# The first value block between the two key blocks, and the output product split around the second eight heads' sums, in a two-layer trunk

## The chip, the cores and the metric

One core of one Trainium2 chip. The metric is device time in microseconds for one execution of the whole program (both layers, 256 frames); lower is better. Before the change: 611.75 us, the median of 3 runs (611.36 to 612.37).

## What is computed

A trunk of two layers on `x` of 256 frames by 1024, float32. Layer 0 mixes frames by differential attention, layer 1 by sparse attention with a choice of keys; each mixer and each MLP (4096 wide, squared ReLU) is preceded by an RMS norm and followed by a residual. The change is in layer 1's mixer:

```python
def dsa_attention(h, w_in, cq_g, w_uq, w_uq_idx, q_g, k_g, w_out, cos, sin):
    proj = h @ w_in
    c_q, k, v, k_idx, w_idx = split(proj)          # 256, 1024, 1024, 64, 8 columns
    c_q = rms_norm(c_q, cq_g)
    q = c_q @ w_uq                                 # 16 heads of 64
    q_idx = rope(c_q @ w_uq_idx)                   # 8 index heads of 64
    k_idx = rope(rms_norm(k_idx))
    q = rope(rms_norm(q, q_g)) * 64 ** -0.5
    k = rope(rms_norm(k, k_g))
    # per block of 128 queries
    score = einsum('bqh,bqhk->bqk', w_idx, relu(q_idx . k_idx))   # masked by chunks of 64
    vals, idx = top_k(score, 64)
    s = q . k[idx]
    p = softmax(s over the chosen keys)
    return (p @ v[idx]) @ w_out
```

The kernel doesn't gather: it turns the top-k choice into a mask over all keys (`smask`) and computes dense scores.

## The kernel before, in words

**Precision by three products.** Every float32 weight matrix is streamed from memory in units of 128 x 2048 (1 MB). `unit` (L126) loads one to `raw` on SP's queue, makes its rounded part `whi` on ScalarE (L141) and the rest `wlo` on VectorE (L142), in two pieces of 1024 columns each. There are three `raw` buffers and four of `whi` and `wlo`, so a unit's split waits until the matmuls on the unit four places before it are done. A product is then three matmuls into one PSUM bank (`mm3`, L145; L146, L148, L150). `project` (L236) multiplies the normed input `h` by one block of 512 columns: two units, 48 matmuls of 512 columns. An `acc` PSUM bank is held for each of the two row tiles.

**Order of the weights.** `_weights` lays the units out in the order of their use: for the sparse layer the index and compressed-query columns, keys 0, keys 1, the query matrix (one unit), values 0, values 1, the output matrix (four units), then the MLP.

**Sparse attention.** `compress` and `index` (L676) compute the index queries and keys, their scores (L732) and the choice: for each of two query tiles eight rounds of a maximum of eight (L741) and its removal (L742) on VectorE. Meanwhile `project` makes keys 0 and 1 (each eight heads) and the query matrix gives queries 0 and 1 (one unit, 12 matmuls for each eight heads, 24 in all). After each, `qk_post` (L347) copies PSUM to `qn` (L354), squares (L356), reduces (L357), scales the keys (L364), applies rotary (L342 to L345, on VectorE), transposes on TensorE (L374) and copies the result (L377). `qn` has two buffers.

Then, for each half of the heads, `dsa_probs` (L771) takes four pairs of heads: score matmuls (L390), mask and minimum (L401), exponential on ScalarE (L412), division (L786, L788), transposes (L419) and copies to `aT` (L421). `dsa_out` (L791) multiplies by the values `vt` (L799, L800) and splits the result into the output product's operand `o` (L804 on ScalarE, L805 on VectorE); one call covers four heads, two calls one half. `v_part` (L554) projects one half of the values and copies it to `vt` (L558). `out_proj` (L430) multiplies `o` by the output matrix unit by unit: units 0 and 1 need the first half's `o`, units 2 and 3 the second's; each unit is 24 matmuls. Before each unit it drives the generators listed for it to their end (`needs`).

**What sets the order.** Python generators (`spawn`, `need`, `tick`, L92 to L118) fix the order in which instructions are traced; `PAUSE` (L41) gives the number of matmuls after which a waiting piece is traced. The framework then writes each engine's list at build time: an instruction traced earlier goes first among those that it takes to be ready, so an engine's list is not the traced order. On the chip every engine works through its list in order. The order traced before, for the sparse layer: keys 0 and their post-work, keys 1 and theirs, queries 0, queries 1, then for each half: probabilities, value block of that half, weighted sums; then the output product. The lines just there are

```python
    for half in range(2):
        aTs = []
        probs = spawn(dsa_probs(half, aTs))
        v_part(half, h, srow)
        need(probs)
        for i in range(2):
            dsa_out(2 * half + i, aTs[4 * i:4 * i + 4])
    h = new_h()
    out_proj(o, take() + take(), h, C_NORM + 24)
```

Of the kernel before, what the change touches and what calls it, by code (L numbers as in the profile page):

```python
# [25 lines left out]
C_NORM = 0  # L26
# [10 lines left out]
            0.0014142135623842478, 0.00027424818836152554, 5.3182957344688475e-05, 1.0313385246263351e-05]  # L37

PAUSE = {"idx scores 1": 1, "idx transposes 0": 1, "idx transposes 1": 36, "q1 transposes 0": 1,  # L41
         "out0": 1, "out1": 2, "out2": 24, "out3": 27}
# [3 lines left out]
def trunk(ctx: ExitStack, tc: tile.TileContext, x_in, pos_in, pack_in, wf, out):  # L46
# [13 lines left out]
    def acc():  # L60
        return psum.tile([128, 512], F32, name="acc", bufs=4)
# [36 lines left out]
    def advance(e, to_end=False):  # L98
        was, inside[0] = inside[0], True
        while e in side and (to_end or e[0] <= 0):  # L100
            try:
                e[0] = next(e[1])
            except StopIteration:
                side.remove(e)
        inside[0] = was

    def spawn(gen):
        e = [0, gen]
        side.append(e)
        advance(e)  # L110
        return e

    def need(*es):
        for e in es:
            advance(e, True)
# [10 lines left out]
    def unit(cols=2048, dmas=1, pieces=1, between=None):  # L126
        raw = wraw.tile([128, 2048], F32, name="raw")
        hi = wsp.tile([128, 2048], F32R, name="whi")
        lo = wsp.tile([128, 2048], F32R, name="wlo")
        src = bass.AP(tensor=wf.tensor, offset=wf.offset + off[0], ap=[[cols, 128], [1, cols]])  # L130
        off[0] += 128 * cols
        step = cols // dmas
        for i in range(dmas):
            c = slice(i * step, (i + 1) * step)
            nc.sync.dma_start(raw[:, c], src[:, c])
            if between is not None and i == 0:
                between()
        step = cols // pieces
        for i in range(pieces):
            c = slice(i * step, (i + 1) * step)  # L140
            nc.scalar.activation(hi[:, c], raw[:, c], AF.Copy)  # L141
            nc.vector.tensor_tensor(lo[:, c], raw[:, c], hi[:, c].bitcast(F32), op=OP.subtract)  # L142
        return hi[:, :cols], lo[:, :cols]

    def mm3(ps, ah, al, wh, wl, first, last):  # L145
        mm(ps, ah, wh, start=first, stop=False)  # L146
        tick()
        mm(ps, ah, wl, start=False, stop=False)  # L148
        tick()
        mm(ps, al, wh, start=False, stop=last)  # L150
        tick()
# [79 lines left out]
    def lhs(h, kt, t):  # L231
        hi, lo = h[kt // 4][:2]
        c = slice(t * 128, t * 128 + 128)
        return hi[:, kt % 4, c], lo[:, kt % 4, c]
# [195 lines left out]
    def out_proj(o, us, h, gc, needs=((),) * 4):  # L430


        ps = [[acc() for _ in range(2)] for _ in range(2)]
        for u, (wh, wl) in enumerate(us):
            need(*needs[u])
            wh = wh.rearrange("p (k n) -> p k n", n=D)
            wl = wl.rearrange("p (k n) -> p k n", n=D)
            for n in range(2):
                for t in range(2):
                    c = slice(n * 512, n * 512 + 512)  # L440
                    for i in range(2):
                        k = u * 2 + i
                        ah, al = lhs(o, k, t)
                        mm3(ps[t][n], ah, al, wh[:, i, c], wl[:, i, c], k == 0, k == 7)
                    if u == 3:
                        for j in range(2):
                            c = slice(n * 512 + j * 256, n * 512 + j * 256 + 256)
                            nc.vector.tensor_tensor(x[t][:, c], ps[t][n][:, j * 256:j * 256 + 256], x[t][:, c],
                                                    op=OP.add)
                            make_h(h, gc, t, n, (j,))  # L450
# [71 lines left out]
    h = new_h()  # L522
# [8 lines left out]
    srow, s2 = row_scale(1)  # L531
# [22 lines left out]
    def v_part(half, h, srow):  # L554
        ps = [acc() for _ in range(2)]
        project(ps, h, quad(take()), 512)
        for t in range(2):
            nc.scalar.activation(vt[:, t, half * 512:half * 512 + 512], ps[t], AF.Copy, scale=srow[:, t:t + 1])  # L558

    o = new_h()  # L560
# [60 lines left out]
    def take():  # L621
        return ready.pop(0) if ready else pair()

    pr = [[] for _ in range(4)]
    probs, outs = [], []
# [11 lines left out]
    h = new_h()  # L637
# [3 lines left out]
    h = h1  # L641
# [15 lines left out]
    srow, s2 = row_scale(2)  # L657
# [93 lines left out]
    def post(res, *a):  # L751
        res += yield from qk_post(*a)

    posts = []
    for n in range(2):
        ps = [acc() for _ in range(2)]
        project(ps, h, quad(take()), 512)
        posts.append(spawn(post(kTs[n], ps, s2c, scon, 3, 1, 0, (C_GT + 3, C_GT + 3), f"k{n}")))
    uq = [a.rearrange("p (k n) -> p k n", n=D) for a in unit(pieces=2)]
    for n in range(2):  # L760
        ps = [acc() for _ in range(2)]
# [7 lines left out]
    o = new_h()  # L769

    def dsa_probs(half, out):  # L771

        need(chosen, posts[half], posts[2 + half])
        rs = qTs[half][2]
        z = tiny.tile([128, 8, 2], F32, name="dz")
        st = {}
        for p in range(5):
            yield pause(f"probs {half}{p}")
            if p < 4:
                st[p] = scores(qTs[half][p // 2], kTs[half][p // 2], p % 2, smask)  # L780
            if p > 0:
                for r, (s, mn) in enumerate(st.pop(p - 1)):
                    hd = 2 * p - 2 + r
                    e = expo(s, mn, rs[:, :, hd], [z[:, hd, t:t + 1] for t in range(2)])
                    rz = tiny.tile([128, 2], F32, name="rz")
                    nc.vector.reciprocal(rz, z[:, hd])  # L786
                    for t in range(2):
                        nc.vector.tensor_scalar(e[:, TS[t]], e[:, TS[t]], rz[:, t:t + 1], None, op0=OP.mult)  # L788
                    out.append(to_keys(e))

    def dsa_out(g, aTs):  # L791
        ops = wk()
        for p in range(2):
            c = p * 256
            for r in range(2):
                rows = slice(64 * r, 64 * r + 64)
                a = aTs[2 * p + r]
                vc = (4 * g + 2 * p + r) * 64
                mm(ops[rows, c:c + 256], vt[:, 0, vc:vc + 64], a[:, 0:256], start=True, stop=False)  # L799
                mm(ops[rows, c + 128:c + 256], vt[:, 1, vc:vc + 64], a[:, 256:384], start=False, stop=True)  # L800
        k = 2 * g
        oh = o[k // 4][0][:, k % 4:k % 4 + 2].rearrange("p a b -> p (a b)")
        ol = o[k // 4][1][:, k % 4:k % 4 + 2].rearrange("p a b -> p (a b)")
        nc.scalar.activation(oh, ops, AF.Copy)  # L804
        nc.vector.tensor_tensor(ol, ops, oh.bitcast(F32), op=OP.subtract)  # L805

    for half in range(2):
        aTs = []
        probs = spawn(dsa_probs(half, aTs))
        v_part(half, h, srow)  # L810
        need(probs)
        for i in range(2):
            dsa_out(2 * half + i, aTs[4 * i:4 * i + 4])
    h = new_h()
    out_proj(o, take() + take(), h, C_NORM + 24)

    def store(t, n, j):
        if (t, n) != (1, 1) and j == 0:
# [13 lines left out]
def _weights(i):  # L832

    parts = []
    w = i["diff_w_in"][0]
    q, k, v = w[:, :1024], w[:, 1024:2048], w[:, 2048:]

    def add(m, rows):
        for r in range(0, m.shape[0], rows):
            parts.append(_tiles(m[r:r + rows]))  # L840

    def a(j):
        add(np.concatenate([q[:, 256 * j:256 * j + 256], k[:, 256 * j:256 * j + 256]], axis=1), 512)

    def mlp(w1, w2):
        def up(b):
            for s in range(2):
                parts.append(_tiles(w1[:, 512 * b + 256 * s:512 * b + 256 * s + 256]))

        up(0)  # L850
        for b in range(8):
            if b < 7:
                up(b + 1)
            add(w2[512 * b:512 * b + 512], 256)

    a(0)
    a(1)
    a(2)
    a(3)
    add(v[:, :512], 512)  # L860
    add(v[:, 512:], 512)
    add(i["diff_w_out"][0], 256)
    mlp(i["mlp_w1"][0], i["mlp_w2"][0])
    w = i["dsa_w_in"][0]
    c = np.concatenate([w[:, :256], w[:, 2304:]], axis=1)
    parts.append(_tiles(c[:768]))
    parts.append(np.concatenate([_tiles(m).reshape(128, -1) for m in (c[768:], i["dsa_w_uq_idx"][0])], axis=1).reshape(-1))
    add(w[:, 256:768], 512)
    add(w[:, 768:1280], 512)
    parts.append(_tiles(i["dsa_w_uq"][0]))  # L870
    add(w[:, 1280:1792], 512)
    add(w[:, 1792:2304], 512)
    add(i["dsa_w_out"][0], 256)
    mlp(i["mlp_w1"][1], i["mlp_w2"][1])
    return np.concatenate(parts)
# [44 lines left out]
```

## Time and profile before

| | |
|---|---|
| runs | 611.36, 611.75, 612.37 us |
| the profiled execution | 611.71 us, its span 609.2 us |
| TensorE (PE) busy | 595.2 us, 98% of the span |
| VectorE (DVE) busy | 428.7 us, 70% |
| ScalarE (ACT) busy | 368.5 us, 60% |
| GpSimd (POOL) busy | 15.9 us, all in the first 50 us |
| sparse attention | about 308 to 426 us of the span |

PE's busy time is modelled from overlapping matmuls, so the distance between the starts of neighbouring matmuls says more than their durations. In a row of the timeline the first number is the start, the second the length, `xN` merges N neighbours, and the bracket at the end is the idle time before it and what ended it.

### The profile page before, as it was taken

The numbers are of one execution on the slowest core, as the hardware profiler recorded it, in microseconds if no ns is written. First come the engines' busy times: TensorE is split into PE (matmuls) and PEld (weight loads), VectorE is DVE, ScalarE is ACT, GpSimd is POOL, SyncE is SP. The second block draws the span as 40 slices with busy tenths as digits, with TensorE's granted clock in tenths as the row PEclk, the third lists the DMA queues.
The fourth block names the chain that finished last, engine by engine and source line by source line (L and its number), as shares of the span: only waits on it lengthen the run. The fifth ranks groups of instructions, "written<-read, shape, count | busy, mean of one in ns | idle before, by whom it ended". The sixth has DMA issues, their size and how long they took to land.

```text
span 609.2 us, 8462 instructions
## 1 busy us (share of the span) xinstructions
PE 595.2 (98%) x3064; PEld 490.0 (80%) x3064; DVE 428.7 (70%) x1067; ACT 368.5 (60%) x720; POOL 15.9 (3%) x53
## 2 busy tenths in 40 slices
PE   8899999999999999999999899999999999999997
PEld 7677768888888888888787686768888888888886
DVE  5698986489566567557588999775886566665552
ACT  6788987577445445444397579794854454455430
POOL 5400000000000000000000000000000000000000
PEclk9899999999999999999999999999999999999999
DMA  8464343435645554554554216414475555555301
GB/s 314 180 257 165 138 157 132 176 109 210 218 176 207 205 165 183 208 192 149 197 178 169 70 69 207 140 69 139 139 230 194 197 206 169 186 200 203 143 1 69
DMA packets 16025, 102.29 MB, mean 168 GB/s; under 512 B 1904, under 2 KB 2416, under 8 KB 4336
## 3 DMA queue, kind: packets, MB, share of 16 engines
q1 hardware_dynamic: 15696, 101.62, 47.5%
q8 instruction: 24, 0.39, 0.3%
q10 hardware_dynamic: 288, 0.13, 0.1%
q14 instruction: 17, 0.14, 0.1%
HBM read 100.70 MB, written 1.05 MB: 167 GB/s over the span
## 4 chain that ended last, share of the span: by engine, by line
PE 82%; DVE 10%; ACT 3%; POOL 2%; issue 2%; DVEq 0%; POOLq 0%; ACTq 0%
PE wk L469 18%; PE acc L150 15%; PE acc L148 15%; PE acc L146 15%; PE wk L470 9%; DVE wlo L142 4%; DVE s L401 2%; PE wk L419 2%; PE acc L469 1%; PE wk L390 1%; PE wk L223 1%; ACT whi L141 1%; PE wk L374 1%; PE acc L470 1%; DVE score L742 1%
## 5 line engine op out<-in xcount | busy, mean ns | idle before, releaser
L142 DVE TENSOR_TENSOR wlo<-raw,whi 128x1024 fp32r<-128x1024 f32 (+2 forms) x210 | 229.8, 1116 | 119.1 <-ACT whi L141 118.9
L141 ACT ACTIVATE whi<-raw 128x1024 fp32r<-128x1024 f32 (+2 forms) x210 | 197.8, 974 | 95.4 <-issue 46.1
L146 PE MATMUL acc<-whi,act 128*128 128x512 f32 (+1 forms) x504 | 200.7, 399 | 2.0 <-ACT whi L141 2.0
L148 PE MATMUL acc<-wlo,act 128*128 128x512 f32 (+1 forms) x504 | 199.2, 395 | 0.8 <-DVE wlo L142 0.8
L150 PE MATMUL acc<-whi,act 128*128 128x512 f32 (+1 forms) x504 | 199.2, 395 | 0.0
L469 PE MATMUL wk<-act,whi 128*128 128x512 f32 x480 | 169.5, 397 | 0.0
L470 PE MATMUL wk<-act,wlo 128*128 128x256 f32 x480 | 134.5, 280 | 0.0
L146 PEld LDWEIGHTS acc<-whi,act 128*128 128x128 f32 x504 | 96.1, 191 | 21.9 <-ACT whi L141 2.4
L148 PEld LDWEIGHTS acc<-wlo,act 128*128 128x128 f32 x504 | 95.9, 190 | 20.2 <-DVE wlo L142 1.4
L150 PEld LDWEIGHTS acc<-whi,act 128*128 128x128 f32 x504 | 96.0, 190 | 19.5 <-issue 1.0
L469 PEld LDWEIGHTS wk<-act,whi 128*128 128x128 f32 x480 | 90.1, 188 | 21.9
L470 PEld LDWEIGHTS wk<-act,wlo 128*128 128x128 f32 x480 | 90.6, 189 | 0.5
L478 ACT ACTIVATE act<-on 128x256 fp32r<-128x256 f32 x64 | 26.3, 416 | 57.6 <-DVE on L477 57.6
L412 ACT ACTIVATE s<-s,nb,rs_r 128x128 f32<-128x128 f32 x64 | 34.2, 537 | 8.2 <-DVE nb L410 8.1
L479 DVE TENSOR_TENSOR act<-on,act 128x256 fp32r<-128x256 f32 x64 | 26.7, 423 | 14.5 <-ACT act L478 12.7
L475 ACT ACTIVATE sq<-wk 128x256 f32<-128x256 f32 x60 | 22.4, 375 | 17.5 <-PE wk L470 17.5
L477 DVE SCALAR_TENSOR_TENSOR on<-sq 128x256 f32<-128x256 f32 x64 | 26.6, 420 | 0.9
L476 DVE TENSOR_TENSOR sq<-wk,sq 128x256 f32<-128x256 f32 x60 | 24.8, 417 | 0.0
L227 ACT ACTIVATE act<-wk,pack 128x128 fp32r<-128x128 f32 x64 | 18.4, 376 | 8.7 <-PE wk L223 8.6
L229 DVE SCALAR_TENSOR_TENSOR act<-wk,pack,act 128x128 fp32r<-128x128 f32 x64 | 18.0, 343 | 3.8 <-ACT act L227 3.6
L419 PE MATMUL wk<-pack,s 128*128 128x128 f32 x72 | 15.7, 290 | 2.4 <-DVE s L580 1.6
L517 DVE SCALAR_TENSOR_TENSOR x<-acc,rows,x 128x256 f32<-128x256 f32 x16 | 7.0, 479 | 15.1 <-PE acc L150 15.1
(176 smaller groups left out, 431.6 us busy)
## 6 DMA issues: line engine op xcount, KB each, us to landing
raw<-in_w SPq DMA_DIRECT2D x91, 1024.0 KB, 4.8
x<-in_x SPq DMA_DIRECT2D x4, 256.0 KB, 4.6
raw<-in_w SPq DMA_DIRECT2D x4, 256.0 KB, 5.3
raw<-in_w SPq DMA_DIRECT2D x2, 512.0 KB, 5.4
raw<-in_w SPq DMA_DIRECT2D x1, 984.0 KB, 4.7
raw<-in_w SPq DMA_DIRECT2D x1, 840.0 KB, 4.6
out_dram<-x SPq DMA_DIRECT2D x3, 256.0 KB, 2.0
out_dram<-x SPq DMA_DIRECT2D x2, 128.0 KB, 1.8
```

The costliest lines, as they stand in the source:

```text
L141: nc.scalar.activation(hi[:, c], raw[:, c], AF.Copy)
L142: nc.vector.tensor_tensor(lo[:, c], raw[:, c], hi[:, c].bitcast(F32), op=OP.subtract)
L146: mm(ps, ah, wh, start=first, stop=False)
L148: mm(ps, ah, wl, start=False, stop=False)
L150: mm(ps, al, wh, start=False, stop=last)
L412: nc.scalar.activation(p[:, TS[t]], s[:, TS[t]], AF.Exp, bias=nb[:, t:t + 1], scale=nsc[:, t:t + 1], accum_out=z[t])
L419: nc.tensor.transpose(pt[:, i * 128:(i + 1) * 128], p[:, i * 128:(i + 1) * 128], ident)
L469: mm(ps.rearrange("p (a b) -> p a b", b=256), wh[:, k, c], both[:, :, k % 4], start=k == 0, stop=False)
L470: mm(ps[:, 256:], wl[:, k, c], hi[:, k % 4], start=False, stop=k == 7)
L477: nc.vector.scalar_tensor_tensor(q, r, 0.0, r, op0=OP.max, op1=OP.mult)
L478: nc.scalar.activation(uh[:, m], q, AF.Copy)
L479: nc.vector.tensor_tensor(ul[:, m], q, uh[:, m].bitcast(F32), op=OP.subtract)
```

## The change

In the sparse layer values 0 are projected directly behind keys 0 and ahead of keys 1, with their weights moved to that place in the stream. Values 1 follow the first half's probabilities as traced. The second half's weighted sums become a generator `rest` that pauses until it is called for; the output product calls for it ahead of its third unit, so that units 0 and 1 are traced ahead of those sums. Computation and instructions are otherwise the same.

```diff
+NEVER = 1 << 30
...
         posts.append(spawn(post(kTs[n], ps, s2c, scon, 3, 1, 0, (C_GT + 3, C_GT + 3), f"k{n}")))
+        if n == 0:
+            v_part(0, h, srow)
...
-    for half in range(2):
-        aTs = []
-        probs = spawn(dsa_probs(half, aTs))
-        v_part(half, h, srow)
+    aTs = [[], []]
+    probs = spawn(dsa_probs(0, aTs[0]))
+    v_part(1, h, srow)
+    need(probs)
+    for i in range(2):
+        dsa_out(i, aTs[0][4 * i:4 * i + 4])
+    probs = spawn(dsa_probs(1, aTs[1]))
+
+    def rest():
+
+
+        yield NEVER
         need(probs)
         for i in range(2):
-            dsa_out(2 * half + i, aTs[4 * i:4 * i + 4])
+            dsa_out(2 + i, aTs[1][4 * i:4 * i + 4])
+
+    last = spawn(rest())
     h = new_h()
-    out_proj(o, take() + take(), h, C_NORM + 24)
+    out_proj(o, take() + take(), h, C_NORM + 24, ((), (), (last,), ()))
...
     add(w[:, 256:768], 512)
+    add(w[:, 1280:1792], 512)
     add(w[:, 768:1280], 512)
     parts.append(_tiles(i["dsa_w_uq"][0]))
-    add(w[:, 1280:1792], 512)
     add(w[:, 1792:2304], 512)
```

## Rows read from the trace of the kernel before

**Rows 1.** The page's first lines: busy time and share of the span of TensorE, and the granted clock in 40 slices, in tenths.

```profile
PE 595.2 (98%) x3064; PEld 490.0 (80%) x3064; DVE 428.7 (70%) x1067; ACT 368.5 (60%) x720; POOL 15.9 (3%) x53
...
PEclk9899999999999999999999999999999999999999
```

**Rows 2.** All waits of PE from 310 to 430 us: us in total, times, longest.

```profile
PE wk L374 <- DVE qn L345: 2.2, 1, 2.2
PE wk L419 <- DVE s L788: 0.7, 2, 0.5
PE wk L390 <- DVE act L805: 0.4, 1, 0.4
```

**Rows 3.** Windows around the long wait: length, then busy us (and instructions) of PE, weight loads, DVE, ACT, POOL, then granted clock, DMA share, GB/s.

```profile
345.30:347.42 2.12, 0.00 (x1) 0.03 (x1) 2.12 (x11) 0.00 (x0) 0.00 (x0) 1.00 0.26 108
347.42:348.00 0.58, 0.58 (x4) 0.53 (x5) 0.58 (x2) 0.00 (x0) 0.00 (x0) 1.00 0.00 0
348.00:351.40 3.40, 3.40 (x10) 2.65 (x9) 3.40 (x15) 2.93 (x4) 0.00 (x0) 0.50 0.02 5
```

**Rows 4.** PE's timeline from the end of keys 0 (334.44) over keys 1 and the queries; the last row is the first after the queries.

```profile
334.44 0.39 PE L150 MATMUL acc<-whi,act 128*128 128x512 f32 x1
334.66 0.39 PE L146 MATMUL acc<-whi,act 128*128 128x512 f32 x1
...
344.86 0.39 PE L146 MATMUL acc<-whi,act 128*128 128x512 f32 x1
347.42 0.41 PE L374 MATMUL wk<-pack,qn 128*128 128x128 f32 x2 [2.17 <-DVE qn L345]
347.59 0.48 PE L148 MATMUL acc<-wlo,act 128*128 128x512 f32 x1
...
349.51 0.63 PE L146 MATMUL acc<-whi,act 128*128 128x512 f32 x1
349.94 0.63 PE L148 MATMUL acc<-wlo,act 128*128 128x512 f32 x1
...
352.89 0.39 PE L150 MATMUL acc<-whi,act 128*128 128x512 f32 x1
...
355.86 0.39 PE L146 MATMUL acc<-whi,act 128*128 128x512 f32 x1
```

**Rows 5.** VectorE's timeline over the first keys' rotary step (L342 to L345) and what stands between.

```profile
345.47 0.28 DVE L342 TENSOR_TENSOR rp<-qn,rc 128x128 f32<-128x128 f32 x1
345.67 0.42 DVE L741 MAX8 m<-score 128x8 f32<-128x256 f32 x1
...
347.06 0.21 DVE L345 TENSOR_TENSOR qn<-rp,rp 128x64 f32<-128x64 f32 x1
```

**Rows 6.** Windows by stage, columns as in rows 3.

```profile
355.40:365.76 10.36, 10.36 (x54) 8.33 (x52) 10.03 (x36) 7.93 (x16) 0.00 (x0) 1.00 0.28 101
365.76:388.75 22.99, 22.40 (x126) 17.10 (x125) 21.21 (x85) 21.03 (x54) 0.00 (x0) 1.00 0.62 210
...
391.55:409.40 17.85, 17.24 (x96) 12.05 (x94) 13.98 (x69) 13.88 (x43) 0.00 (x0) 1.00 0.17 60
```

**Rows 7.** ScalarE's timeline: splits of weights (L141), a projection's square (L356), the last copy of values (L558) and the last of the first heads' probabilities (L421).

```profile
322.05 1.07 ACT L141 ACTIVATE whi<-raw 128x1024 fp32r<-128x1024 f32 x1
...
354.88 0.63 ACT L356 ACTIVATE sq<-qn 128x512 f32<-128x512 f32 x1
...
381.30 1.99 ACT L141 ACTIVATE whi<-raw 128x1024 fp32r<-128x1024 f32 x2
...
387.81 0.68 ACT L558 ACTIVATE vt<-acc,srow 128x512 f32<-128x512 f32 x1
388.38 0.49 ACT L421 ACTIVATE aT<-wk 128x384 f32<-128x384 f32 x1
```

**Rows 8.** PE's timeline: score matmuls, transposes, the first weighted sum, the first output matmul among the second heads' work, and the second half's sums.

```profile
365.76 1.58 PE L390 MATMUL wk<-qkT 64*128 64x128 f32 x16
367.27 0.50 PE L150 MATMUL acc<-whi,act 128*128 128x512 f32 x1
...
387.79 1.04 PE L374 MATMUL wk<-pack,qn 128*128 128x128 f32 x8
388.75 0.66 PE L799 MATMUL wk<-aT,vt 128*64 128x256 f32 x4
...
393.74 0.49 PE L146 MATMUL acc<-whi,act 128*128 128x512 f32 x1
...
409.41 0.65 PE L799 MATMUL wk<-aT,vt 128*64 128x256 f32 x2
```

**Rows 9.** Weight splits on VectorE, grouped: in 355.3 to 365.76 us, and in 365.76 to 388.75 us (busy us, mean ns).

```profile
L142 DVE TENSOR_TENSOR wlo<-raw,whi 128x1024 fp32r<-128x1024 f32 x2 | 2.4, 1216 | 0.0
...
L142 DVE TENSOR_TENSOR wlo<-raw,whi 128x1024 fp32r<-128x1024 f32 x9 | 10.8, 1210 | 0.0
```

**Rows 10.** VectorE's timeline: the last rescaling of the first eight heads, then the split ahead of the copy of their sums.

```profile
386.73 0.55 DVE L788 TENSOR_SCALAR s<-s,rz 128x128 f32<-128x128 f32 x2
391.01 1.23 DVE L142 TENSOR_TENSOR wlo<-raw,whi 128x1024 fp32r<-128x1024 f32 x1 [3.73 <-ACT whi L141]
392.15 0.68 DVE L805 TENSOR_TENSOR act<-wk,act 128x512 fp32r<-128x512 f32 x1
```

**Rows 11.** The weight transfers on SP's queue from 310 to 440 us: size and median us to landing.

```profile
raw<-in_w SPq DMA_DIRECT2D x17, 1024.0 KB, 4.9
```

## The prediction

> **What bounds the kernel now.** The page first: TensorE is busy 98% of the span and its clock is granted in full nearly everywhere [rows 1]. So a change of order can only win back the few us in which PE waits or is slowed, and it can lose by making new ones. Next the waits of PE in the sparse attention (310 to 430 us): one of 2.17 us and some 1.1 us in all the rest [rows 2]. The windows around the large one show what it costs beyond itself: PE stands still from 345.30 to 347.42, and for the next 3.4 us the granted clock is 0.50, the 1.2 GHz level [rows 3]. The timeline of PE gives the step of one 512-column matmul at either level: from 334.66 to 344.86 there are 45 steps, 0.227 us each; at the lower level the start moves by 0.427 (349.51 to 349.94) [rows 4]. Eight slow steps, 8 x 0.20 = 1.6 us. Wait and slow clock together: 3.7 us.
>
> The same timeline says what PE waits for. The first key projection's last matmul is at 334.44. Then come 46 matmuls of the second one, and the two transposes of the first keys stand ahead of its last two (from 347.59), which need nothing from the transposes and wait with them [rows 4]. The transposes wait for the rotary step of the first keys on VectorE, whose instructions are spread over 345.47 to 347.27 because pieces of the top-k choice stand between them [rows 5].
>
> After that PE runs without a gap until 365.76, and from there to 388.75 its idle time is 22.99 - 22.40 = 0.6 us [rows 6]. But this cover is just enough: in 365.76 to 388.75 the first eight heads' probabilities run on ScalarE (busy 21.0 of 23.0 us) and VectorE (21.2), while PE fills with the value projections. The second value block is finished only at the end: its last copy out of PSUM stands at 387.81, and the last probabilities are copied at 388.38 [rows 7]. Three engines end together.
>
> **The change part by part.** The sum is made against the profiled execution, 611.71 us with a span of 609.2; the median of the runs is 611.75, so the two agree to 0.04. About 0.2%, 1.2 us, is what a measurement can tell from no change.
>
> *Work.* No instruction is added or removed: both value blocks, all projections and all heads stay. In the weight stream one pair of 1 MB units moves ahead of three others of the same size; SP's queue issues the same 1 MB transfers, 4.9 us each [rows 11], and POOL's issues none. Cost 0: the pair behind the first keys was rounded on ScalarE by 323.1, eleven us before its first matmul at 334.66 [rows 7, 4], and the place in the stream decides that, not the content. If that cover were gone, a pair would cost its 4.9 us of landing and two splits.
>
> *The stretch up to 348 us.* The block that follows the first keys has 48 matmuls of 512 columns in either kernel. Behind the first keys' end, PE still gets 46 ready matmuls, then the two transposes; on VectorE the top-k choice and the first keys' normalisation are untouched. I take the wait and the slow clock as they are: 0. Bounds: 0, or -3.7 if the order moves the transposes back by 2.17 / 0.227 = 10 matmuls.
>
> *Cover moved.* 48 x 0.227 = 10.9 us of PE work go from behind the query projections to ahead of the second keys. The first queries, whose last matmul starts at 352.89 [rows 4], end 10.9 us later, near 364, and everything behind them moves likewise: the second queries, done at 355.86, to 366.8, then only one value block of fill instead of two. PE's own work from 366.8: 10.9 (values) + 24 transposes of keys and queries at 0.12 (eight from 387.79 to 388.75) + 32 score matmuls at 0.094 (16 from 365.76 to 367.27) + 24 transposes of probabilities at about 0.12 [rows 8], in all 19.7, end 386.5 where before it was 388.75. So PE's floor is -2.2 us; of that I allow 1.0 for changing between kinds of matmul, floor -1.2.
>
> Whether the floor is reached is decided on VectorE. In 355.40 to 388.75 it was busy 10.03 + 21.21 = 31.2 us [rows 6], of which weight splits took 2.4 + 10.8 = 13.2 [rows 9]; the other 18.0 are the second keys' remainder, both queries and the first eight heads. In the changed kernel the second keys end on PE 24 matmuls after that same 355.86, near 361.3, and reach VectorE after two ScalarE passes of 0.6 each (the square: 0.63, [rows 7]), near 362.5, and bring 0.6 more (a reduction that was done earlier). So 362.5 + 18.6 = 381.1, plus the splits that run in between. Each split waits for its buffer, and there are four; the output weights' first three units get theirs when the second keys (361.3), the second queries (366.8) and half of the last value block (about 374, with the transposes) are done, thus six pieces of 1.13 = 6.8 (before, these same six also ran ahead of the end; the last pair's rounding is at 381.30 [rows 7]). That gives 387.9, and with 1.5 us of waiting (before 2.1 of 33.3) 389.4, against a last rescaling that ended at 387.28 before [rows 10]: **+2.1 us**. Bounds: with none of the splits in the way VectorE would end at 382.6 and PE's floor holds, -1.2; with eight pieces and the waits of before, 392.2, +5.0. I take six, since the splits ran as soon as their buffers came in the kernel before.
>
> *Weights out of the way later.* The last output unit's split stood between the first heads' output product and its own copies: split 391.01, copy 392.15 [rows 10], and PE waited 0.41 for that copy [rows 2]. Its buffer now comes free before, when the value block ends: **-1.1 us**, the length of one piece; bounds 0 and -1.9.
>
> *First half of the output product beside the second eight heads.* It stands there already: output matmuls begin at 393.74, between the score matmuls of the second heads, and run up to the second sums at 409.41 [rows 8]. Gain 0. What changes is rank: the second heads' weighted sums (from 409.41) are now traced behind the 48 matmuls of this half; before, those left over covered the copies that follow the sums. Without them the third unit waits for such a pair of copies (0.68 on VectorE [rows 10], about as much on ScalarE, 1.3 together), of which the second sum, some half of 409.41 to 413, hides the larger part: **+0.5 us**; bounds 0 and +1.3.
>
> Sum: 2.1 - 1.1 + 0.5 = +1.5, 611.71 + 1.5 = **613.2 us**.
>
> **The clock in the thinned stretch.** With one block of fill, PE has no large matmuls from about 384 on, only transposes with waits between. In the kernel before, one full stop of 2.1 us was followed by 3.4 us at 0.50 [rows 3], while stretches with waits of 0.4 us kept 1.00 [rows 2, 6]. My waits lie between. The Trainium skill (TensorE: Matmul & The Clock Gate, section Loop structure matters more than you think) asks that fill be laid out so that matmuls follow one another without long waits, since the engine else goes cold; the trace agrees with its 2.1 us stop. By that rule the sum would be 614.8, by the short waits of the rows it stays at 613.2.
>
> **The rivals.**
> 1. *The clock falls* in the uncovered tail: the sum + 1.6 = 614.8. For it: at 389 PE lacks some 3 to 4 us of work. Against: the lack is split among the last heads.
> 2. *No change.* VectorE skips some splits (four pieces instead of six, 4.5: 387.1 with the waits), so that the cover term shrinks to about 0: 0 - 1.1 + 0.5 = -0.6, 611.1. For it: a split can wait where the heads are ready.
> 3. *Faster through the tail.* The splits are done early, PE's floor -1.2 is reached: -1.2 - 1.1 + 0.5 = -1.8, 609.9. For it: between the end of the top-k choice and 361 VectorE has few other tasks. Against: 18.6 us of head work start only at 362.5.
> 4. *Faster through the stop at 345 us.* With the values behind the first keys, their transposes are placed 10 or more matmuls later and neither stop nor slow clock occurs: -3.7 + 1.5 = -2.2, 609.5. It decides when the first keys' transposes stand behind at least 56 matmuls instead of 46. For it: it is the one large loss here, and 96 ready matmuls would stand behind the first keys. Against: before, 48 of keys and 24 of queries stood there too, and the transposes were put behind 46.
>
> **How the numbers follow.** Forecast 0.34; clock 0.12; no change 0.26; faster through the tail 0.17; through the stop 0.11. Slower: 0.34 + 0.12 = 0.46, same 0.26, faster 0.17 + 0.11 = 0.28. The forecast's own range is 612.9 (cover term +1.8) to 616.1 (+5.0). Range for all: down to 607.8, rival 4 with half of what rival 3 has over the forecast (609.5 - 1.7), and up to 617.0, the forecast's upper end with some half of the slow clock (616.1 + 0.9).
>
> **What would show it.** Right: a PE wait near 2 us before the first keys' transposes, still at 347 us and followed by 0.50; value matmuls from 334.7; the first score matmuls of the heads near 371 to 373; PE waits on the rescaling or on ScalarE's copies of several us between 380 and 391; no split between output product and copies. Wrong: no stop at 345 us, or value matmuls still filling PE when the eighth head's probabilities are copied. The prediction fails if VectorE ends the first heads by 387.

## The result: 1.5% slower, and the profile after

Median 620.79 us (4 runs, 619.77 to 621.62) against 612.06 for the kernel before beside it: ratio 1.0145, interval 1.0131 to 1.0158, a loss of 8.7 us. The profiled execution took 619.96 us, its span 617.7 (before 609.2).

The page after, first lines (as in [rows 1]):

```profile
span 617.7 us, 8468 instructions
...
PE 598.7 (97%) x3064; PEld 491.4 (80%) x3064; DVE 429.9 (70%) x1067; ACT 370.1 (60%) x720; POOL 16.0 (3%) x53
...
PEclk8899999999999999999999999699999999999999
```

This is already the whole loss. TensorE runs the same 3064 matmuls, busy 3.5 us longer (598.7 - 595.2) and idle 5.0 us longer (617.7 - 598.7 = 19.0 against 14.0): 8.5 us, the growth of the span. The clock row shows where: one slice at 6 tenths, at 386 to 401 us. Its waits from 310 to 445 us (as in [rows 2]):

```profile
PE wk L420 <- DVE s L791: 5.3, 4, 1.7
PE wk L375 <- DVE qn L346: 2.2, 1, 2.2
PE wk L391 <- DVE act L808: 0.3, 1, 0.3
```

The second row is the old stop. The first is new: transposes of probabilities wait for the rescaling. TensorE's timeline, answering [rows 4, 8]:

```profile
348.33 0.41 PE L375 MATMUL wk<-pack,qn 128*128 128x128 f32 x2 [2.17 <-DVE qn L346]
...
369.68 0.41 PE L375 MATMUL wk<-pack,qn 128*128 128x128 f32 x2
...
371.51 0.41 PE L375 MATMUL wk<-pack,qn 128*128 128x128 f32 x2
...
373.15 0.82 PE L375 MATMUL wk<-pack,qn 128*128 128x128 f32 x6
...
374.58 1.58 PE L391 MATMUL wk<-qkT 64*128 64x128 f32 x16
...
381.03 0.39 PE L151 MATMUL acc<-whi,act 128*128 128x512 f32 x1
...
382.60 0.81 PE L420 MATMUL wk<-pack,s 128*128 128x128 f32 x4 [1.18 <-DVE s L791]
...
386.62 0.30 PE L420 MATMUL wk<-pack,s 128*128 128x128 f32 x1 [1.09 <-DVE s L791]
...
390.66 1.51 PE L420 MATMUL wk<-pack,s 128*128 128x128 f32 x6 [1.36 <-DVE s L791]
...
393.85 1.54 PE L420 MATMUL wk<-pack,s 128*128 128x128 f32 x4 [1.68 <-DVE s L791]
...
397.45 0.80 PE L802 MATMUL wk<-aT,vt 128*64 128x256 f32 x4
```

The stop of 2.17 stays. Transposes of keys 1 (from 369.68) and of queries 0 (from 371.51) now come together, and the first scores stand right behind, at 374.58 instead of 365.76. The last value matmul is at 381.03; from there to the first sum at 397.45 the four waits lie. Windows, columns as in [rows 3]: behind the stop, 372 to 400 us, and the low clock in the tail.

```profile
348.40:352.00 3.60, 3.60 (x19) 2.84 (x20) 3.60 (x14) 2.58 (x3) 0.00 (x0) 1.00 0.00 0
372.00:400.00 28.00, 22.57 (x129) 16.51 (x129) 20.10 (x89) 23.38 (x59) 0.00 (x0) 0.82 0.34 114
387.60:397.80 10.20, 7.05 (x29) 5.04 (x30) 5.82 (x24) 8.10 (x23) 0.00 (x0) 0.50 0.31 104
```

The same 28 us of the kernel before:

```profile
372.00:400.00 28.00, 27.00 (x165) 20.13 (x163) 22.47 (x82) 23.60 (x61) 0.00 (x0) 1.00 0.50 170
```

165 matmuls then, 129 now. Behind the stop the clock stayed at 1.00; in the tail it was at 0.50, the 1.2 GHz level, for 10.2 us. VectorE's splits and the last rescaling of the first eight heads (as in [rows 10]), and its window from the first of those splits to that rescaling's end:

```profile
362.57 1.23 DVE L143 TENSOR_TENSOR wlo<-raw,whi 128x1024 fp32r<-128x1024 f32 x1 [1.95 <-ACT whi L142]
364.57 1.22 DVE L143 TENSOR_TENSOR wlo<-raw,whi 128x1024 fp32r<-128x1024 f32 x1
371.47 1.23 DVE L143 TENSOR_TENSOR wlo<-raw,whi 128x1024 fp32r<-128x1024 f32 x1
373.69 1.23 DVE L143 TENSOR_TENSOR wlo<-raw,whi 128x1024 fp32r<-128x1024 f32 x1
379.80 2.35 DVE L143 TENSOR_TENSOR wlo<-raw,whi 128x1024 fp32r<-128x1024 f32 x2
387.24 1.23 DVE L143 TENSOR_TENSOR wlo<-raw,whi 128x1024 fp32r<-128x1024 f32 x1 [0.51 <-ACT whi L142]
391.22 1.22 DVE L143 TENSOR_TENSOR wlo<-raw,whi 128x1024 fp32r<-128x1024 f32 x1
394.57 0.55 DVE L791 TENSOR_SCALAR s<-s,rz 128x128 f32<-128x128 f32 x2
...
399.84 0.69 DVE L808 TENSOR_TENSOR act<-wk,act 128x512 fp32r<-128x512 f32 x1 [4.72 <-ACT act L807]
```

```profile
362.57:395.12 32.55, 26.95 (x135) 19.53 (x135) 29.33 (x120) 28.43 (x69) 0.00 (x0) 0.88 0.39 129
```

In the timeline, eight pieces stand ahead of the last rescaling (395.12) and none between the sums and their copy at 399.84.

By stage: the first scores come 8.82 us later, from there to the first sum it takes 22.87 us against 22.99, from the first sum to the end of the span 220.25 against 220.46. Of the 8.82 us, 0.91 were there ahead of the moved block: the first projection matmul behind the index scores starts at 333.17 against 332.26. The order is the same up to there; this execution had a lower clock at its start (mean granted clock 0.91 in the first 40 us, against 0.96).

### The profile page after: what moved, and what is told of

Read it like the earlier page. It is cut to its first block, busy times and chain, and to the rows that moved or that the text cites. A ratio compares the mean times of both kernels' runs of the same rounds, so it can differ in the third digit from the quotient of the medians.

```text
span 617.7 us, 8468 instructions
## 1 busy us (share of the span) xinstructions
PE 598.7 (97%) x3064; PEld 491.4 (80%) x3064; DVE 429.9 (70%) x1067; ACT 370.1 (60%) x720; POOL 16.0 (3%) x53
## 4 chain that ended last, share of the span: by engine, by line
PE 81%; DVE 12%; ACT 2%; POOL 2%; issue 2%; DVEq 0%; POOLq 0%
PE wk L470 18%; PE acc L151 15%; PE acc L147 15%; PE acc L149 15%; PE wk L471 9%; DVE wlo L143 4%; DVE s L402 2%; PE wk L420 2%; PE wk L391 1%; PE acc L470 1%; PE wk L224 1%; PE wk L375 1%; ACT whi L142 1%; DVE qkss L358 1%; PE wk L802 1%
## 5 line engine op out<-in xcount | busy, mean ns | idle before, releaser
L420 PE MATMUL wk<-pack,s 128*128 128x128 f32 x72 | 17.0, 318 | 7.1 <-DVE s L791 5.3
L420 PEld LDWEIGHTS wk<-pack,s 128*128 128x128 f32 x72 | 9.1, 152 | 15.5 <-DVE s L791 4.9
```

Of the source, the lines that this page charges most:

```text
L420: nc.tensor.transpose(pt[:, i * 128:(i + 1) * 128], p[:, i * 128:(i + 1) * 128], ident)
```

## The experiments

**Which part loses.** First part alone; second part alone.

```diff
 e1 = before +     if n == 0: v_part(0, h, srow)      # and the stream's order
 e2 = before +     last = spawn(rest())               # and out_proj's needs
```

> Only the first part of the change: values 0 between keys 0 and keys 1 (with their weights), the second half's sums as before. Theory (the moved block delays the first heads' chain, nothing else matters): 620 to 621.5 us, all of the loss. Rival (the rank of the second half's sums behind 48 output matmuls costs a part): below 619.5.

620.84 us, ratio 1.0143 (1.0125 to 1.0160).

> Only the second part: values 0 back behind the queries, the second half's sums called for by the output product at its third unit. Theory: 611 to 613 us, as before, since the output product's first half ran beside the second eight heads already. Rival (rank costs): above 613.5.

611.36 us, 0.9991 (0.9979 to 1.0003). The loss is the first part's, all of it.

**Less and more for TensorE.** The changed kernel without the moved block (its heads use values that were never projected), and with values 1 projected twice.

```diff
 e3: -        if n == 0:
     -            v_part(0, h, srow)
 e4: +    v_part(1, h, srow, 2)     # 48 more matmuls behind the queries
```

> The changed kernel with the first value block left out altogether (its weights too; the values of the first eight heads are then stale). Theory (in the kernel before this block costs nothing, it only fills the chain's waiting; in the changed one it is paid in full): 620.8 - 10.9 = 609.9, about 2 us under the kernel before, in range 608.5 to 612. Rival (VectorE's load sets the end of the first heads, 2.3 us of splits leave with the block and PE was the floor before): 605 or below.

616.07 us, 1.0060 (1.0042 to 1.0078): 10.9 us of matmuls less than the kernel before, and slower than it, above the expected range. TensorE waits 7.9 us for the rescaling and sits at 0.50 for 20.5 us.

> The changed kernel with the second value block projected twice into the same banks, 48 matmuls or 10.9 us of PE work more, behind the queries. Theory (PE lacks fill there while a chain of steps runs): most of the 10.9 us is hidden, 620 to 625 us, and with the clock held at 1.00 perhaps no more than now. Rival (throughput of PE): 631 us. If the low clock of the tail is itself a large part of the loss, the time falls below 620.

623.04 us, 1.0169 (1.0148 to 1.0191): 48 matmuls more cost 2.2 us. So the changed kernel has a hole behind the queries that takes about 48 - 2.2 / 0.227 = 38 matmuls. With it filled the clock stays at 1.00 there and the waits for the rescaling shrink from 5.3 to 0.4 us.

**Where the block stands.** Behind keys 1 (e5), between queries 0 and 1 (e6), and as before but with queries 0 behind keys 0 (e7).

```diff
 e5: +        if n == 1:
     +            v_part(0, h, srow)      # behind keys 1
 e6: +        if n == 0:
     +            v_part(0, h, srow)      # behind queries 0
 e7:  order: keys 0, queries 0, keys 1, queries 1
```

> The changed kernel with values 0 one place later: behind keys 1 and still ahead of the query matrix. Theory (what counts is that the first eight heads' queries come 10.9 us later): the same loss, 618.5 to 622 us. Rival (the loss is the meeting of keys 1 and the queries on VectorE near 362 to 372 us, since keys 1 were moved too): keys 1 are then done early, 613 to 616.

614.04 us, 1.0037 (1.0021 to 1.0053): the time of the rival, not of the theory. Late queries 0 alone are not the loss.

> The changed kernel with values 0 between queries 0 and queries 1. Theory: the first eight heads' chain starts as in the kernel before, 611 to 613.5 us. Rival (any place ahead of the second queries costs): above 616.

614.02 us, 1.0035 (1.0018 to 1.0052), between the two expected ranges.

> The kernel before with queries 0 ahead of keys 1 (keys 0, queries 0, keys 1, queries 1, values 0, values 1; the query matrix moves up in the stream), the opposite of the change: the first eight heads' inputs are ready 10.9 us earlier. Theory: their chain then starts when the top-k choice is done, near 355 instead of 365.8, and 10.9 us of fill more stand beside it; 607 to 611 us. Rival (VectorE's load sets the start): 611 to 614.

611.84 us, 1.0006 (0.9989 to 1.0024). In e5 queries 0 are transposed from 367.74, late too, at a loss of only 2.4 us; but keys 1 are transposed from 360.65, well before them. In e7 the last transposes of queries 0 start at 357.96 and are copied by 359.94, but the scores still stand at 367.33, right behind the first transposes of keys 1 (367.02), which the first eight heads don't use.

**Delays.** Keys 0's transposes traced later in the kernel before (e8), keys 1's post-work later in the changed kernel (e10), the choice of keys later in the kernel before (e12).

```diff
 e8:  PAUSE = {... +"k0 transposes 0": 58,
 e10: PAUSE = {... +"k1 post": 13,          # and a yield pause(...) ahead of it
 e12: PAUSE = {... +"idx choice 0": 14,
```

> The kernel before with the transposes of keys 0 traced 58 matmuls after keys 0 instead of at once. If the stop of 2.17 us and the 3.4 us of slow clock behind it are a matter of the transposes' place: 3.7 us less, 608 us. If VectorE's delay of keys 0 returns as a wait later: 611 to 613.

622.38 us, 1.0169 (1.0148 to 1.0191). A miss as a test of the stop: keys 0's transposes were bundled with keys 1's and the one wait grew to 8.31 us.

> The changed kernel with the post-work of keys 1 traced 13 matmuls later, that is behind the post-work of queries 0, which alone the first eight heads wait for. If the loss beyond the moved block is their meeting on VectorE: first score matmuls 2 to 4 us earlier, 614 to 618 us. If not: 620 to 622.

622.56 us, 1.0185 (1.0163 to 1.0206). Transposes of queries 0 at 366.0, of keys 1 at 376.2, the scores again behind the later, at 376.51. Queries 0 were copied by 369.46, so here the scores stood 7 us behind transposes that they don't need.

> The kernel before with the top-k choice traced behind the post-work of keys 0, so that keys 0 go first on VectorE; the choice is needed only at the heads' scores. The transposes of keys 0 then stand behind 36 matmuls. If the stop of 2.17 us comes from the choice between their steps: no stop, and without the slow clock behind it 608 to 610 us. If it stays: 611 to 613.

612.87 us, 1.0027 (1.0014 to 1.0040). In the profiled execution, the slowest of the twelve (614.91), the stop is still 1.9 us, followed by 3.4 us at 0.50.

**Extra matmuls against the low clock** (e11: six 128-column matmuls behind each of the first eight heads' copies, results unused).

```diff
+        for _ in range(extra):
+            mm(pt[:, 384:512], o[:, 0:128], o[:, 128:256], start=True, stop=True)
```

> The changed kernel with six extra 128-column matmuls (0.1 us each at the full clock) after each of the first eight heads' copies, into unused columns of the bank: 5 us of PE work more, result unused. If the low clock in the thinned stretch costs something of its own and the work holds the clock up: 617 to 620 us. If the clock stays low or costs nothing: 621 to 626.

625.13 us, 1.0219 (1.0198 to 1.0240). The low clock of the tail falls to 3.4 us, but each matmul stands behind a copy, and from first exponential to last rescaling it takes 18.6 us instead of 15.4. So this run says nothing of the clock's price.

**The heads ahead of keys 1.** Queries 0 and the first heads' probabilities traced ahead of keys 1: in the kernel before (e9), and with the value block in its new place (e13).

```diff
 for n in range(2):
     ... keys n
+    if n == 0: v_part(0, h, srow)                    # e13 only
     ... queries n
+    if n == 0: probs[0] = spawn(dsa_probs(0, aTs[0]))
```

> Queries 0 behind keys 0 as in the run that moved them, and the first eight heads' probabilities traced right there, ahead of keys 1, so that both key 1 and both value blocks may fill. If their late start in that run (first score matmuls 7 us after the queries' copies) was the rank of keys 1 in the trace: first score matmuls near 360 us, and 607 to 610.5 us in all. If VectorE's other work holds them: 611 to 613.

612.31 us, 1.0019 (1.0007 to 1.0032). The first scores come at 358.22, 7.5 us earlier than before and 9.1 us earlier than in e7, which differs from e9 only in where the first heads are traced. So in e7 the order held them. Nothing is won by it: there was little idle time of TensorE to win (0.59 us in that stretch before, 0.35 now).

> The block of values stays behind keys 0 as in the changed kernel, but queries 0 and the first eight heads are put into the program ahead of keys 1, so that their scores need not stand behind the transposes of keys 1 in TensorE's order (the output's first half is handled as in the kernel before). Theory (the loss is that four projections, not three, stand ahead of the first scores): first scores near 367, first sum near 390, 611 to 614 us. Rival (a block ahead of the queries costs its time wherever the scores stand, because half the fill is gone): first sum 396 or later, 618 us or more.

611.27 us, 0.9995 (0.9985 to 1.0006). The block is where the change put it, and the loss is gone. (The output's first half is handled as before here; by e2 that is worth nothing.) TensorE's waits in e13, 310 to 430 us, then its window of 372 to 400 us:

```profile
PE wk L374 <- DVE qn L345: 2.2, 1, 2.2
PE wk L419 <- DVE s L773: 0.3, 1, 0.3
```

```profile
372.00:400.00 28.00, 28.00 (x164) 21.80 (x163) 25.37 (x90) 26.23 (x61) 0.00 (x0) 1.00 0.28 96
```

No idle time in those 28 us, full clock, 164 matmuls. And this is how the kernels stand in one table; fill is the number of 512-column projection matmuls between the first scores and the first sum, stretch the time between the two (us, profiled runs):

| | first scores | fill | stretch | PE idle in it | first sum | span |
|---|---|---|---|---|---|---|
| before | 365.76 | 61 | 22.99 | 0.59 | 388.75 | 609.2 |
| after | 374.58 | 22 | 22.87 | 5.43 | 397.45 | 617.7 |
| e5 | 370.85 | 34 | 19.47 | 2.49 | 390.32 | 610.6 |
| e9 | 358.22 | 52 | 21.91 | 0.35 | 380.13 | 608.9 |
| e13 | 360.79 | 79 | 28.42 | 0.25 | 389.21 | 609.0 |

The change takes 61 - 22 = 39 matmuls out of the stretch, 39 x 0.227 = 8.9 us that now run ahead of it, and the stretch doesn't get shorter. In e5 27 leave it, and it gets 3.5 us shorter.

**VectorE's sum** (e14: values 1's low parts on GpSimd; e15: the first output pair's too; e16: both value blocks' in the kernel before).

```diff
-            nc.vector.tensor_tensor(lo[:, c], raw[:, c], ...
+            ve.tensor_tensor(lo[:, c], raw[:, c], ...        # ve = nc.gpsimd for these units
```

> The changed kernel with the four low parts of the second value block's weights (VectorE at 362.6, 364.6, 371.5 and 373.7, 1.2 us each) computed on GpSimd. Theory that VectorE's sum sets the end of the stretch: keys 1 and queries 0 are ready up to 4.9 us earlier, the first sum comes near 393, 616 to 617 us. Rival (the order and the waits between the engines set it, VectorE's sum does not): scores at 374 to 375 as before, 619.5 to 621 us; slower than 622 if GpSimd's pieces come late for the fill.

622.08 us, 1.0168 (1.0141 to 1.0195).

> As the run before, and the four pieces of the output product's first weights (VectorE at 379.8 twice, 387.2 and 391.2) on GpSimd too: all eight pieces have left VectorE. Theory of VectorE's sum: first sum near 389 to 390, 612 to 614 us. Rival (order and waits): the chain from first exponentials to last rescale stays above 14 us and the time above 618 us.

631.1 us, 1.0297 (1.0272 to 1.0321).

> The control for the two: the kernel before with both value blocks' low parts on GpSimd. If the first heads of the kernel before are bound by VectorE too, the first sum comes up to 4 us earlier and the time is 608 to 610 us; if by TensorE's order, 611 to 612 us; if GpSimd is late with a piece, over 613 us.

626.17 us, 1.0238 (1.0220 to 1.0257). The three runs don't settle whether VectorE's sum sets the end of the stretch, since moving the pieces made VectorE itself slower. VectorE's and then GpSimd's timeline in e14:

```profile
350.85 2.31 DVE L346 TENSOR_TENSOR qn<-rp,rp 128x64 f32<-128x64 f32 x1
...
353.42 3.06 DVE L143 TENSOR_TENSOR wlo<-raw,whi 128x1024 fp32r<-128x1024 f32 x1
...
356.81 1.21 DVE L143 TENSOR_TENSOR wlo<-raw,whi 128x1024 fp32r<-128x1024 f32 x1
```

```profile
350.73 4.67 POOL L143 TENSOR_TENSOR wlo<-raw,whi 128x1024 fp32r<-128x1024 f32 x2 [325.64 <-ACT whi L142]
```

While GpSimd works on its pieces, 2.4 us each, a rotary instruction of 64 columns takes 2.31 us instead of 0.22, and a split 3.06 instead of 1.21. Keys 1's transposes slip to 373.1 in e14 and 376.0 in e15.

**The stop once more.** e17 is e13, e18 the changed kernel, both with keys 0's transposes 57 matmuls behind keys 0.

```diff
 PAUSE = {... +"k0 transposes 0": 57,
```

> The run with queries 0 and the first heads ahead of keys 1, and the transposes of keys 0 put 57 matmuls behind keys 0 instead of where they stop TensorE for 2.17 us: eleven more matmuls of the value block go in front of them. If the stop is a true cost, it goes, with it what the low clock behind it took (1.7 us in that run), and the time is 607.5 to 609.5 us, below the kernel before. If TensorE only waits elsewhere instead, 611 us.

611.37 us, 0.9985 (0.9975 to 0.9996): at most 0.25% below the kernel before, not the 2 to 4 us expected.

> The changed kernel with the same later place of keys 0's transposes. If the stop is lost time in it as well, 618 to 619 us. If the first heads' wait for keys 1 and queries 0 is fixed by VectorE and ScalarE and not by how early TensorE ends their projections, the 2 us are given back as waits in the heads: 620 to 621 us.

621.12 us, 1.0141 (1.0128 to 1.0155). TensorE's timeline in e17 shows why neither tells what a vanished stop is worth:

```profile
348.34 0.38 PE L374 MATMUL wk<-pack,qn 128*128 128x128 f32 x2
348.48 0.48 PE L146 MATMUL acc<-whi,act 128*128 128x512 f32 x1
351.21 0.87 PE L374 MATMUL wk<-pack,qn 128*128 128x128 f32 x6 [2.25 <-DVE qn L345]
```

The first two transposes no longer wait; the other six do, for the second half of the frames, whose rotary step ends 3 us later. The stop has moved.

The stretch from the first scores to the first sum in the changed kernel, in e18 and in e5, columns as in [rows 3]:

```profile
374.58:397.45 22.87, 17.44 (x87) 12.36 (x86) 17.36 (x81) 19.51 (x52) 0.00 (x0) 0.78 0.42 139
374.59:398.55 23.96, 19.10 (x87) 13.17 (x87) 17.35 (x81) 19.60 (x52) 0.00 (x0) 0.70 0.38 133
370.85:390.32 19.47, 16.98 (x100) 12.24 (x99) 14.95 (x77) 16.41 (x48) 0.00 (x0) 1.00 0.17 56
```

## Why the prediction was wrong

The direction was right, and the loss lies in the term that was named for it, the moved cover; its size was wrong: +1.5 us forecast, +8.7 measured, above the range.

- **The stop kept at 0: right.** 2.17 us at 348.33, rival 4 is out. The clock stayed at 1.00 behind it, though 0.50 was forecast, which hides 1.6 us of this execution's loss. That belongs to the execution and not to the order: e4 and e11, the same up to there, have 3.4 us at 0.50 behind the same stop, and e2, in this part the same as the kernel before, has none.
- **Cover moved, +2.1: this step failed.** It let VectorE end the first heads at 389.4 (26.9 us from 362.5: 18.6 + 6.8 + 1.5); it ended at 395.12. The window 362.57 to 395.12 is 32.55 us, 5.6 more, and all three terms were short: eight split pieces, 9.7 us in place of six in 6.8 (+2.9, of which 0.5 because the prediction took splits off at 1.21 each and put them back at 1.13); other work 29.3 - 9.7 = 19.6 in place of 18.6 (+1.0); waits 3.2 in place of 1.5 (+1.7). From that end to the first sum it took 2.3 us, before 1.5. The eight pieces were in the bounds (+5.0), but together with few waits. The first scores came at 374.58, not at 371 to 373. The deeper error is the floor for TensorE, set 1.2 us below the time of before. It counted work and not order: it took TensorE to fill the stretch, but 26 of the last block's 48 matmuls ran ahead of the scores, and with the other 22 TensorE stood idle for 5.43 us of it.
- **The cause.** e1 shows that the block's place is the whole loss, e4 that the stretch behind the first scores lacks some 38 matmuls (39 left it), and e13 that the same place costs nothing once queries 0 and the first heads stand ahead of keys 1. In the changed kernel the first scores follow keys 1 and queries 0 in TensorE's list, so with the block ahead of both they wait for four projections instead of three, and one is left to run beside them. That count is not all of it, for in e5 four stand ahead too. There queries 0 are copied out of PSUM at the same time (the second copy at 365.13, against 365.36 in the changed kernel), but keys 1 are through by then. In the changed kernel keys 1 and queries 0 come together on VectorE: queries 0 are transposed from 371.51 instead of 367.74, their transposed copies start at 373.68, and the scores begin right behind the first of these, 3.73 us later than in e5. The stretch behind them is 3.40 us longer than in e5, with 22 matmuls to fill it instead of 34, and with 10.1 us at 0.50 instead of none. e10 shows that freeing queries 0 alone doesn't help, since the scores then stand behind keys 1 in TensorE's list; e13 takes both holds away.
- **Rival 1, the clock falls (0.12): it came in addition**, three times as long: 10.2 us at 0.50 with TensorE busy 7.05 in them. 7.05 / 2 = 3.5 us would be its worth if all of it were work at half speed, as much as TensorE's busy time grew. What the path pays is not shown: e4 has no low clock there, but its TensorE is full, and e11 brought a chain of its own. An estimate comes from e18, whose first scores (374.59) and 22 matmuls of fill are those of the changed kernel: its stretch has a mean granted clock of 0.70 instead of 0.78, 14.4 us at 0.50 instead of 10.1, and takes 23.96 us instead of 22.87. At 1.1 us for 4.3, the 10.1 us would be worth some 2.5 of the 8.7. The prediction weighed the Trainium skill (TensorE: Matmul & The Clock Gate, section Loop structure matters more than you think) against the rows and went by short waits that had kept the full clock. In the thinned tail waits of 1.1 to 1.7 us came with the low clock, so there the trace agrees with the Trainium skill.
- **Last split out of the way, -1.1, and rank of the second sums, +0.5: small together, as forecast.** No split stands before the copies, TensorE waits 0.3 us for them, and from the first sum on the kernel takes 0.2 us less (forecast 0.6). The two were not measured apart. The output's first half won nothing, as forecast: e2.

Open: why the same stop of 2.17 us is followed by 3.4 us of low clock in some executions and by none in others; how the 8.7 us divide between late scores, thin fill and the low clock; and whether VectorE's sum or the order sets the length of the stretch.

## What to carry to other kernels

Where one engine is busy 98%, price a move by what it leaves beside each stretch whose length another chain sets: here 39 matmuls left a stretch of 23 us that did not get shorter, and nearly their whole time was lost. How much shorter such a stretch gets has to be asked each time: where 27 left it (e5), 2.4 us were lost. Look in the engine's list for what a chain stands behind without needing it, before moving work in front of it. Handing pieces to an idle engine has to be priced by what that engine takes from its neighbour.

## What was not expected of the hardware

- Less work, same order, slower than before: e3 leaves out 10.9 us of matmuls and pays with 7.9 us of waits and 20.5 us at the low clock.
- While GpSimd subtracted, VectorE's instructions took longer: 2.31 us for one of 0.22, about the length of GpSimd's own piece (2.35 to 2.41), in e14. The Trainium skill (SBUF — State Buffer, section Who interferes with whom) says that a VectorE instruction with two SBUF inputs contends with a GpSimd instruction that reads SBUF, and calls the shared port pair an exclusive lock. e14's rows agree.
